# The first stretch of layer 0: x by single feature tiles, query products between key and value products

## The chip, the cores and the metric

The kernel runs on one core of one Trainium2 chip, in one launch. The metric is the time of one execution on the device, in microseconds (us); the number that is compared is the median of repeated executions. A profile of one execution lies beside the times: it gives the start and the length of every instruction on TensorE (PE, with its weight loads as PEld), VectorE (DVE), ScalarE (ACT), GpSimd (POOL) and SyncE (SP, which here only issues DMA transfers).

## The reference

Two layers of a decoder trunk over 512 tokens of 1024 features, in float32. The change touches only the beginning of layer 0, cut here to what it computes:

```python
h = _rms_norm(x, mix_norm[0])
q, k, v, cb, cc, cx = _split(h @ w_in, (512, 128, 128, 512, 512, 512))
q = _apply_rope(_rms_norm(q.reshape(b, s, 8, 64), q_norm), cos, sin)
k = _apply_rope(_rms_norm(k.reshape(b, s, 2, 64), k_norm), cos, sin)
attn = _sliding_window_sink_attention(q, k, v, sinks)
conv = cb * _causal_depthwise_conv(cc * cx, conv_w)
x = x + jnp.concatenate([attn, conv], axis=-1) @ w_out
```

The token's factor of the norm (one over its root mean square) is left out of h in the kernel and put on the finished products.

## The kernel before

Every float32 product is made of three matmuls in a rounded format: each operand is split into a rounded part (made by ACT, names `wh` for weights and the first `a` for x) and a rest (made by DVE, `wl` and the second `a`); rounded times rounded, rounded times rest and rest times rounded are summed in one PSUM bank. A helper `mm3` issues the three in a row.

In the first stretch of `mixer0`, x comes as rows of tokens (tiles `xin`) and has to be turned so that features lie on the partitions: PE transposes 128x128 blocks (against the identity, tile `cf`) into a PSUM bank, ACT and DVE read the bank for the two parts of the feature tile, and a third reading keeps x itself in `xT`. There are 8 feature tiles and 4 token tiles. For each feature tile k, the products of keys and values are 4 token tiles x 3 matmuls that give 128x256, those of queries 4 x 3 that give 128x512.

Before the change x is transferred in four pieces of two feature tiles, each as two transfers of 256 KB and followed by 256 KB of key and value weights, all on SP's queue. `features(c)` turns, splits and keeps the two tiles of piece c; `keys_values(k)` runs between them. The query weights come behind all that, as two transfers of 1 MB, and the 96 query matmuls run after the last `keys_values`. Ahead of it all, `idle` gives PE matmuls of ones into a bank that nobody reads: 7 in `setup`, 8 more after the first transposes.

Beside this PE work the chain of the keys runs on the other engines: the squares of x (L529) give the sums of the norm, POOL makes the factor `rtok` of each token (L209), ACT puts it on the key and value products (`kx` L570, `v` L574) and squares them (L543), DVE sums the squares (L545); the positions are turned by one small PE matmul (L418), DVE makes angles of them and, with ACT's sine, the tables `ropeS` and `ropeC` (L424 to L462); DVE combines them into the normed keys `kn` (L549, L554, L579). PE then transposes `kn` (L561), spreads `rtok` (L380) and starts the convolution's products.

Each engine works off its instructions in the order in which they stand. In the first stretch that order is the written one (`manual_schedule`) for PE, DVE and ACT; behind it a scheduler places the instructions of DVE and ACT. Weight tiles `wh` and `wl` have three buffers each, `raw` (weights as they come) has two: whoever writes a buffer again waits for its last reader. A queue's transfers are issued in order, and each waits until the transfer eight before it has landed.

## Time and profile before

| what | value |
|---|---|
| median of 3 runs | 1197.72 us (1196.88 to 1197.98) |
| profiled execution, own time | 1195.99 us |
| span of its instructions | 1194.0 us |
| granted TensorE clock over the span | 1.000 |
| PE from 8.0 to 22.9 us (keys and values) | 14.72 of 14.90 us busy |
| PE from 22.9 to 45.0 us (queries) | 22.10 of 22.10 us busy |
| first key product / first query product | 8.02 us / 23.04 us |
| kn's transposes on PE | 44.96 us |

Times inside the program are microseconds from the start of the span. A row of the timeline shows a start, a length (until the last result is written, so rows of one engine overlap), the engine, the line, the operation, the tile written and the tiles read, and in brackets how long the engine stood idle ahead of it and what ended that. PEq, ACTq, SPq and POOLq are the sequencers that issue transfers.

### The profile page before, as it was taken

Reading aid. Unit: us, or ns where it says so; the run is one execution under the profiler, and the core shown is the slowest. Engines: PE = TensorE matmul, PEld = TensorE weight load, DVE = VectorE, ACT = ScalarE, POOL = GpSimd, SP = SyncE. Lnnn points to the kernel's source line nnn. Section 1 sums busy time; section 2 is a strip of 40 time slices with the busy share of each in tenths; the row PEclk is TensorE's granted clock in tenths of the full one; section 3 lists DMA queues with packets and bytes.
Section 4 is the critical chain, followed back from the end, with each engine's and each line's share of the span. In section 5 each row is a group of like instructions: output and inputs, shape, how many; then the busy total and the mean of one; then the engine's idle time right before and its main releaser. Section 6 shows DMA issues by size and latency. Waiting matters only on the chain.

```text
span 1194.0 us, 20222 instructions
## 1 busy us (share of the span) xinstructions
PE 1187.1 (99%) x8218; PEld 1079.2 (90%) x8218; DVE 993.3 (83%) x1595; ACT 691.6 (58%) x1138; POOL 46.1 (4%) x64
## 2 busy tenths in 40 slices
PE   9999999999999999999999999999999999999998
PEld 8877789999999988889988988899999999888887
DVE  6786687898999987889879876688989999988595
ACT  7466565656565744756664655555555656655374
POOL 2610000000000000000100000000000000000000
PEclk9999999999999999999999999999999999999999
DMA  7222222333323343422412212223232333323601
GB/s 224 72 97 81 74 89 71 107 107 106 107 93 103 113 137 96 130 73 73 139 59 71 89 54 72 88 76 116 92 116 97 106 107 113 126 89 98 211 1 71
DMA packets 113072, 117.76 MB, mean 99 GB/s; under 512 B 2856, under 2 KB 108002, under 8 KB 112980
## 3 DMA queue, kind: packets, MB, share of 16 engines
q1 hardware_dynamic: 112144, 115.88, 29.8%
q8 instruction: 64, 1.05, 0.4%
q0 software_dynamic: 560, 0.42, 0.3%
q14 instruction: 28, 0.23, 0.1%
q10 hardware_dynamic: 276, 0.18, 0.1%
HBM read 114.37 MB, written 2.10 MB: 98 GB/s over the span
## 4 chain that ended last, share of the span: by engine, by line
PE 88%; DVE 8%; ACT 3%; issue 1%; DMA 0%; POOL 0%; ACTq 0%
PE ps L177 8%; PE ps L178 8%; PE ps L179 8%; PE pa L178 6%; PE pa L179 6%; PE pa L177 6%; PE ps L916 5%; PE ps L918 5%; PE ps L917 5%; PE ps L193 5%; PE ps L191 5%; PE ps L200 4%; PE pa L916 2%; PE pa L918 2%; PE pa L917 2%; DVE wl L864 2%
## 5 line engine op out<-in xcount | busy, mean ns | idle before, releaser
L153 DVE TENSOR_TENSOR wl<-raw,wh 128x1024 fp32r<-128x1024 f32 (+3 forms) x138 | 158.6, 1152 | 39.6 <-ACT wh L151 36.5
L151 ACT ACTIVATE wh<-raw 128x1024 fp32r<-128x1024 f32 (+4 forms) x142 | 140.9, 995 | 68.4 <-PE ps L178 26.3
L861 ACT ACTIVATE wh<-raw 128x1024 fp32r<-128x1024 f32 x90 | 95.7, 1063 | 129.5 <-DVE raw L888 79.0
L979 DVE SCALAR_TENSOR_TENSOR zt<-z,vfa,zt 128x510 f32<-128x510 f32 (+1 forms) x176 | 130.8, 744 | 0.3
L864 DVE TENSOR_TENSOR wl<-raw,wh 128x1024 fp32r<-128x1024 f32 x90 | 109.9, 1221 | 17.5 <-ACT wh L861 16.4
L179 PE MATMUL pa<-b,wl 128*128 128x256 f32 x352 | 97.3, 276 | 0.1
L179 PE MATMUL pa<-a,wl 128*128 128x256 f32 x352 | 97.2, 276 | 0.0
L177 PE MATMUL pa<-a,wh 128*128 128x256 f32 x352 | 97.2, 276 | 0.0
L177 PE MATMUL pa<-b,wh 128*128 128x256 f32 x352 | 97.2, 276 | 0.0
L178 PE MATMUL pa<-a,wh 128*128 128x256 f32 x352 | 97.2, 276 | 0.0
L178 PE MATMUL pa<-b,wh 128*128 128x256 f32 x352 | 97.2, 276 | 0.0
L977 ACT ACTIVATE zt<-z,vfb 128x512 f32<-128x512 f32 x88 | 71.3, 810 | 18.3 <-DVE z L969 8.7
L191 PE MATMUL ps<-b,wh 128*128 128x512 f32 (+1 forms) x192 | 73.0, 383 | 0.0
L193 PE MATMUL ps<-b,wh 128*128 128x512 f32 (+1 forms) x192 | 72.3, 379 | 0.0
L179 PEld LDWEIGHTS pa<-b,wl 128*128 128x128 f32 x352 | 66.1, 188 | 0.3 <-DVE wl L153 0.3
L177 PEld LDWEIGHTS pa<-a,wh 128*128 128x128 f32 x352 | 66.1, 188 | 0.0
L177 PEld LDWEIGHTS pa<-b,wh 128*128 128x128 f32 x352 | 66.1, 188 | 0.0
L178 PEld LDWEIGHTS pa<-b,wh 128*128 128x128 f32 x352 | 66.1, 188 | 0.0
L178 PEld LDWEIGHTS pa<-a,wh 128*128 128x128 f32 x352 | 66.1, 188 | 0.0
L179 PEld LDWEIGHTS pa<-a,wl 128*128 128x128 f32 x352 | 66.1, 188 | 0.0
L916 PE MATMUL ps<-four,wh 128*128 128x256 f32 x232 | 64.7, 279 | 0.0
L918 PE MATMUL ps<-four,wl 128*128 128x256 f32 x232 | 64.1, 276 | 0.0
(532 smaller groups left out, 3711.9 us busy)
## 6 DMA issues: line engine op xcount, KB each, us to landing
raw<-in_ffn_w_up_dram SPq DMA_DIRECT2D x42, 1024.0 KB, 5.1
raw<-in_ffn_w_down_dram SPq DMA_DIRECT2D x13, 1024.0 KB, 5.1
raw<-in_hy_w_in_dram SPq DMA_DIRECT2D x8, 1024.0 KB, 4.9
raw<-in_gla_w_in_dram SPq DMA_DIRECT2D x8, 1024.0 KB, 5.2
raw<-in_ffn_w_down_dram SPq DMA_DIRECT2D x8, 768.0 KB, 4.9
raw<-in_ple_w_gate_dram SPq DMA_DIRECT2D x6, 1024.0 KB, 6.5
raw<-in_hy_w_out_dram SPq DMA_DIRECT2D x16, 256.0 KB, 4.0
raw<-in_gla_w_out_dram SPq DMA_DIRECT2D x4, 1024.0 KB, 5.1
```

The source lines that it names most:

```text
L151: nc.scalar.activation(hv, v, AF.Copy)
L153: self.rest_cut = nc.vector.tensor_tensor(lv, v, hv.bitcast(F32), ALU.subtract)
L177: mm(out, lh, rh, start=start, stop=False, **kw)
L178: mm(out, lh, rl, start=False, stop=False, **kw)
L179: mm(out, ll, rh, start=False, stop=stop, **kw)
L191: mm(out, lh, rh, start=first, stop=False, **kw)
L193: end = mm(out, lt, rt, start=False, stop=False, **kw)
L861: nc.scalar.activation(h, src, AF.Copy)
L864: nc.vector.tensor_tensor(l, src, h.bitcast(F32), ALU.subtract)
L916: mm(out, wh, xh, start=first and j == 0, stop=False, **kw)
L918: mm(out, wl, xh, start=False, stop=j == ND // 2 - 1, **kw)
L979: nc.vector.scalar_tensor_tensor(out=y[:, tap:], in0=z[:, : S - tap], scalar=w[:, f : f + 1], in1=y[:, tap:], op0=ALU.mult, op1=ALU.add,)
```

## The change

x comes by one feature tile for the first two tiles (transfers of 128 KB) and by two after that. Weights for queries of the first four feature tiles come on the same queue between the pieces of x, 256 KB for a single tile and 512 KB for two. The first 128 KB of key and value weights are issued by ACT, right behind the identity; the gain vector, which ACT issued, is now issued by POOL. The query products of feature tiles 0 to 3 run between the key and value products; those of tiles 4 to 7 stay behind them. The three matmuls of a product are no longer issued in a row but in passes over the four token tiles. The turned tiles share two PSUM banks, where each had one of four in turn. The idle matmuls are 4 and 3 where they were 7 and 8. Two of the four squares of x stand earlier. What is computed is the same.

```diff
--- before.py
+++ after.py
@@ -217,14 +217,16 @@
         self.ident = self.cf[:, :P]
         self.ones = self.cp.tile([P, P], F32, name="ones")
         self.ones_r = self.sp.tile([P, S + 64], F32R, tag="sq", name="ones_r", bufs=2)[:, :P]
-        self.nowhere = self.pa()
+        self.nowhere = self.ps()
+        self.kvr = self.raw(ND, 256)
         with self.tc.manual_schedule(engines={ET.PE, ET.DVE, ET.Activation}):
             nc.vector.memset(self.ones, 1.0)
             nc.vector.tensor_copy(self.ones_r, self.ones)
             nc.vector.memset(self.mhalf, -0.5)
             nc.scalar.dma_start(self.ident, a["cst_f"][:, :P])
+            nc.scalar.dma_start(self.kvr[:, 0, :], a["hy_w_in"][0][:P, 512:768])
             self.vec0 = self.load_vectors0()
-            self.idle(7)
+            self.idle(4)
         self.invf = self.cf[:, P + 32 : P + 64]
         self.amask = self.cf[:, P + 64 :]
 
@@ -265,7 +267,7 @@
     def load_vectors0(self):
         a = self.a
         f = lambda v: v.rearrange("i (k p) -> (i k) p", p=P)
-        finish = self.columns("vec0", [f(a["mix_norm"])], self.nc.scalar)
+        finish = self.columns("vec0", [f(a["mix_norm"])], self.nc.gpsimd)
 
         def turned():
             v = finish()
@@ -468,65 +470,169 @@
             w_in = a["hy_w_in"][0].rearrange("(k p) n -> p k n", p=P)
             self.xT = [self.xp.tile([P, S], F32, name=f"xT{m}") for m in range(ND)]
             xin = [mp.tile([P, 2, D], F32, tag="s", name=f"xin{u}", bufs=2) for u in range(2)]
-            kvr = self.raw(ND, 256)
-            for c in range(4):
-                cols = slice(c * 256, (c + 1) * 256)
+            kvr, wqr = self.kvr, self.raw(4, 512)
+            load = nc.sync.dma_start
+
+            def load_x(m0, m1):
+                cols = slice(m0 * P, m1 * P)
                 for u in range(2):
                     rows = a["x"][0, u * 256 : (u + 1) * 256, cols]
-                    nc.sync.dma_start(xin[u][:, :, cols], rows.rearrange("(t p) d -> p t d", p=P))
-                nc.sync.dma_start(kvr[:, 2 * c : 2 * c + 2, :], w_in[:, 2 * c : 2 * c + 2, 512:768])
+                    load(xin[u][:, :, cols], rows.rearrange("(t p) d -> p t d", p=P))
+
+            def load_kv(k0, k1):
+                load(kvr[:, k0:k1], w_in[:, k0:k1, 512:768])
+
+            def load_q(k0, k1):
+                load(wqr[:, k0:k1], w_in[:, k0:k1, :512])
+
+            load_x(0, 1)
+            load_q(0, 1)
+            load_x(1, 2)
+            load_kv(1, 2)
+            load_q(1, 2)
+            load_x(2, 4)
+            load_kv(2, 4)
+            load_x(4, 6)
+            load_q(2, 4)
+            load_kv(4, 6)
+            load_x(6, 8)
+            load_kv(6, 8)
             self.gate = xin[1][:, 1, D - 1 :]
             self.late(self.cf[:, P + 32 : P + 33])
             nc.gpsimd.dma_start(self.cf[:, P + 32 :], a["cst_f"][:, P:])
 
             xg = self.xg = []
             tok = lambda k, t: (xg[k][0][:, t * P : (t + 1) * P], xg[k][1][:, t * P : (t + 1) * P])
+            turns = [self.pa(), self.pa()]
             pkv = [self.pa() for _ in range(2)]
             pkv = [pkv[t // 2][:, (t % 2) * 256 : (t % 2) * 256 + 256] for t in range(NT)]
-            wkv = []
-
-            def keys_values(k):
-                for t in range(NT):
-                    self.mm3(
-                        pkv[t], tok(k, t), wkv[k // 2](k % 2, 0, 256),
-                        start=k == 0 and t % 2 == 0, stop=k == ND - 1 and t % 2 == 1,
-                    )
-
-            def features(c, fill=0):
-                ms = (2 * c, 2 * c + 1)
-                pss = [self.ps() for _ in ms]
-                for u in range(2):
-                    if c == 0 and u == 1:
-                        self.vec0()
-                    for m, ps in zip(ms, pss):
-                        for t in (2 * u, 2 * u + 1):
-                            nc.tensor.transpose(
-                                ps[:, t * P : (t + 1) * P], xin[u][:, t % 2, m * P : (m + 1) * P], self.ident
-                            )
-                self.idle(fill)
-                for m, ps in zip(ms, pss):
-                    hl = self.pair(self.fp, "a0", "a1")
-                    self.split(hl, ps, self.g_mix[0][:, m : m + 1])
-                    xg.append(hl)
-                    if m == (c > 0) + 2 * c:
-                        wkv.append(self.cut(kvr[:, 2 * c : 2 * c + 2, :], "a"))
-                return [
-                    copy(self.xT[m], ps) for m, ps, copy in zip(ms, pss, (nc.scalar.copy, nc.vector.tensor_copy))
-                ]
-
-            with tc.manual_schedule(engines={ET.PE, ET.DVE, ET.Activation}):
-                features(0, 8)
-                for c in range(1, 4):
-                    keys_values(c - 1)
-                    last = features(c)
-                for k in range(3, ND):
-                    keys_values(k)
-            wq = [self.weights(w_in[:, k0 : k0 + 4, :512], 4, 512, by="a") for k0 in (0, 4)]
+            psq = [self.ps() for _ in range(NT)]
+            wkv, wq = {}, {}
             sums = self.few(NT, "ss")
             junk = mp.tile([P, D], F32, tag="pT", name="junk")
+            passes = ((0, 0), (1, 0), (0, 1))
+
+            def keys_values(k, *ns):
+                for n in ns:
+                    u, v = passes[n]
+                    for t in range(NT):
+                        nc.tensor.matmul(
+                            pkv[t], tok(k, t)[u], wkv[k][v],
+                            start=k == n == 0 and t % 2 == 0, stop=k == ND - 1 and n == ns[-1] and t % 2 == 1,
+                        )
+
+            def queries(k, *ns):
+                for n in ns:
+                    u, v = passes[n]
+                    for t in range(NT):
+                        nc.tensor.matmul(
+                            psq[t], tok(k, t)[u], wq[k][v], start=k == n == 0, stop=k == ND - 1 and n == ns[-1]
+                        )
+
+            def turn(*ms):
+                for m in ms:
+                    for t in range(NT):
+                        nc.tensor.transpose(
+                            turns[m % 2][:, t * P : (t + 1) * P],
+                            xin[t // 2][:, t % 2, m * P : (m + 1) * P], self.ident,
+                        )
+
+            def rounded_x(m):
+                xg.append(self.pair(self.fp, "a0", "a1"))
+                nc.scalar.activation(xg[m][0], turns[m % 2], AF.Copy, scale=self.g_mix[0][:, m : m + 1])
+
+            def rest_x(m):
+                h, l = xg[m]
+                nc.vector.scalar_tensor_tensor(
+                    out=l, in0=turns[m % 2], scalar=self.g_mix[0][:, m : m + 1], in1=h.bitcast(F32),
+                    op0=ALU.mult, op1=ALU.subtract,
+                )
+
+            def rounded_w(parts, raw, k0, tiles):
+
+                n, w = raw.shape[1:]
+                h, l = (x[:, : n * w].rearrange("p (a b) -> p a b", b=w) for x in tiles)
+                nc.scalar.activation(h, raw, AF.Copy)
+                parts.update({k0 + q: (h[:, q], l[:, q]) for q in range(n)})
+                return lambda: nc.vector.tensor_tensor(l, raw, h.bitcast(F32), ALU.subtract)
+
+            def kept(m, copy):
+                return copy(self.xT[m], turns[m % 2])
+
+            def square(t):
+                nc.scalar.activation(junk, xin[t // 2][:, t % 2, :], AF.Square, accum_out=sums[:, t : t + 1])
+
+            on_act, on_dve = nc.scalar.copy, nc.vector.tensor_copy
+            part = lambda tiles, c0, c1: [x[:, c0:c1] for x in tiles]
+            with tc.manual_schedule(engines={ET.PE, ET.DVE, ET.Activation}):
+                kv01, q01 = self.weight_tiles(), self.weight_tiles()
+                turn(0)
+                self.vec0()
+                self.idle(3)
+                rounded_w(wkv, kvr[:, 0:1], 0, part(kv01, 0, 256))()
+                rounded_x(0)
+                rest_x(0)
+                keys_values(0, 0, 2, 1)
+                rounded_w(wq, wqr[:, 0:1], 0, part(q01, 0, 512))()
+                rest = rounded_w(wkv, kvr[:, 1:2], 1, part(kv01, 256, 512))
+                kept(0, on_act)
+                queries(0, 0)
+                turn(1)
+                rounded_x(1)
+                rest()
+                rest_x(1)
+                rounded_w(wq, wqr[:, 1:2], 1, part(q01, 512, 1024))()
+                kept(1, on_dve)
+                queries(0, 1, 2)
+                keys_values(1, 0, 1, 2)
+                rest = rounded_w(wkv, kvr[:, 2:4], 2, self.weight_tiles())
+                queries(1, 0)
+                turn(2, 3)
+                rounded_x(2)
+                rounded_x(3)
+                rest()
+                rest_x(2)
+                rest_x(3)
+                kept(2, on_act)
+                kept(3, on_dve)
+                queries(1, 1, 2)
+                keys_values(2, 0, 1, 2)
+                rests = [
+                    rounded_w(wkv, kvr[:, 4:6], 4, self.weight_tiles()),
+                    rounded_w(wq, wqr[:, 2:4], 2, self.weight_tiles()),
+                ]
+                turn(4, 5)
+                rounded_x(4)
+                rounded_x(5)
+                for rest in reversed(rests):
+                    rest()
+                rest_x(4)
+                rest_x(5)
+                kept(4, on_act)
+                kept(5, on_dve)
+                keys_values(3, 0, 1, 2)
+                queries(2, 0, 1, 2)
+                rest = rounded_w(wkv, kvr[:, 6:8], 6, self.weight_tiles())
+                square(0)
+                square(1)
+                keys_values(4, 0, 1, 2)
+                turn(6, 7)
+                rounded_x(6)
+                rounded_x(7)
+                rest()
+                rest_x(6)
+                rest_x(7)
+                last = [kept(6, on_act), kept(7, on_dve)]
+                keys_values(5, 0, 1, 2)
+                queries(3, 0)
+                keys_values(6, 0, 1, 2)
+                keys_values(7, 0, 1, 2)
+                queries(3, 1, 2)
+            wq47 = self.weights(w_in[:, 4:8, :512], 4, 512, by="a")
+            wq.update({k: wq47(k - 4, 0, 512) for k in range(4, ND)})
             with tc.issue_after(last[0].ins):
-                for t in range(NT):
-                    nc.scalar.activation(junk, xin[t // 2][:, t % 2, :], AF.Square, accum_out=sums[:, t : t + 1])
+                square(2)
+                square(3)
             self.end_norm(sums=sums)
             with tc.issue_after(last[1].ins):
                 C, Sn = self.rope_tables(mp)
@@ -578,10 +684,9 @@
             kn = mp.tile([P, 8, HD], F32, tag="qn", name="kn", bufs=2)
             nc.vector.tensor_tensor(kn, m1, rk.unsqueeze(2).to_broadcast([P, 8, HD]), ALU.mult)
 
-            psq = [self.ps() for _ in range(NT)]
-            for k in range(ND):
+            for k in range(4, ND):
                 for t in range(NT):
-                    self.mm3(psq[t], tok(k, t), wq[k // 4](k % 4, 0, 512), start=k == 0, stop=k == ND - 1)
+                    self.mm3(psq[t], tok(k, t), wq[k], start=False, stop=k == ND - 1)
             turned(kn, kT, nc.vector.tensor_copy, self.pa)
             qTs = []
 
```

The order of the instructions at three places that are spoken of below.

**PE, from its first instruction to the first key and value product.** `ones_r` holds ones, `cf` the identity, `vrow` the gain vector, `wh`, `wl` and `a` as above. Before:

```order
L235 MATMUL pa_80<-ones_r 128x512 x7
L503 MATMUL ps_132<-cf,xin_111 128x128 x2
L503 MATMUL ps_133<-cf,xin_111 128x128 x2
L259 MATMUL pa_138<-cf,vrow_87 128x16
L503 MATMUL ps_132<-cf,xin_112 128x128 x2
L503 MATMUL ps_133<-cf,xin_112 128x128 x2
L235 MATMUL pa_80<-ones_r 128x512 x8
L177 MATMUL pa_128<-wh_157,a_11_153 128x256
```

And now:

```order
L237 MATMUL ps_80<-ones_r 128x512 x4
L535 MATMUL pa_132<-cf,xin_110 128x128 x2
L535 MATMUL pa_132<-cf,xin_111 128x128 x2
L261 MATMUL pa_152<-cf,vrow_89 128x16
L237 MATMUL ps_80<-ones_r 128x512 x3
L519 MATMUL pa_134<-wh_144,a_21_160 128x256 x2
L519 MATMUL pa_135<-wh_144,a_21_160 128x256 x2
```

Four transposes, one feature tile, stand where eight stood, and seven idle matmuls where fifteen stood.

**PE, around the transpose of the positions** (`pos_f`). Before:

```order
L178 MATMUL pa_129<-wl_270,a_37_265 128x256
L179 MATMUL pa_129<-wh_269,a_38_266 128x256
L418 MATMUL pa_371<-cf,pos_f 128x4
L177 MATMUL ps_448<-wh_338,a_11_153 128x512
L178 MATMUL ps_448<-wl_339,a_11_153 128x512
```

And now:

```order
L528 MATMUL ps_138<-wl_266,a_29_234 128x512
L528 MATMUL ps_139<-wl_266,a_29_234 128x512
L420 MATMUL pa_418<-cf,pos_f 128x4
L177 MATMUL ps_136<-wh_399,a_35_276 128x512
L178 MATMUL ps_136<-wl_400,a_35_276 128x512
```

It stood ahead of all 96 query products; now 48 of them (tiles 0 to 3) stand ahead of it and 48 behind it. Then come the transposes of `kn`, before and now.

**ACT, from the last squares of x to the squares of the keys.** `wh` with `raw` is the rounding of query weights, `kx` and `v` the key and value products with the token's factor. Before:

```order
L529 ACTIVATE junk,ss_356<-xin_112 128x1024 [waits Activation_49]
L151 ACTIVATE wh_348<-raw_346 128x1024 [waits DMAHW7_49,DVE_49,PE_49]
L570 ACTIVATE kx<-pa_128,rtok_362 128x128 [waits Pool_49]
L574 ACTIVATE v_422<-pa_128,rtok_362 128x128
L570 ACTIVATE kx<-pa_128,rtok_362 128x128
```

And now:

```order
L563 ACTIVATE junk,ss_140<-xin_111 128x1024 [waits Activation_49]
L151 ACTIVATE wh_403<-raw_397 128x1024 [waits PE_49]
L676 ACTIVATE kx<-pa_134,rtok_409 128x128 [waits PE_49,Pool_49]
L680 ACTIVATE v_469<-pa_134,rtok_409 128x128
L676 ACTIVATE kx<-pa_134,rtok_409 128x128
```

The places are the same, but the rounding ahead of `kx` now writes the buffer that held the query weights of tiles 2 and 3, whose last reader is the last matmul of `queries(3, 1, 2)`, right ahead of the positions' transpose on PE; before, it wrote a buffer of key and value weights. On DVE the sum of the squared keys (L545, now L651) stood in the middle of the cosine's steps and now stands in the sine's, ahead of its third step. From the transposes of `kn` on, the order of PE is as before, and from the scores of the first query block on, that of all engines.

## The prediction

> **What bounds the kernel now.** I read the page first, then the busy time by stretches, the timeline of PE over the first 45 us, and the timelines of ACT, DVE and POOL up to the keys' transposes.
>
> ```profile
> span 1194.0 us, 20222 instructions
> PE 1187.1 (99%) x8218; PEld 1079.2 (90%) x8218; DVE 993.3 (83%) x1595; ACT 691.6 (58%) x1138; POOL 46.1 (4%) x64
> PE 88%; DVE 8%; ACT 3%; issue 1%; DMA 0%; POOL 0%; ACTq 0%
> ```
>
> ```profile
> 8.00:22.90 14.90, 14.72 (x122) 1.00 0.84 257
> 22.90:45.00 22.10, 22.10 (x99) 1.00 0.37 120
> ```
>
> PE sets the time: it is busy 99% of the span and 88% of the chain that ended last. In the touched stretch it stands still for 0.18 us of 37 (first column the stretch, then its length and PE's busy time). So nothing is to be won there except what PE does that is of no use, and that lies ahead of 8 us:
>
> ```profile
> 1.31 3.35 PE L235 MATMUL pa<-ones_r 128*128 128x512 f32 x7 [1.31 <-DVE mhalf L224]
> 4.47 1.05 PE L503 MATMUL ps<-cf,xin 128*128 128x128 f32 x4
> 5.45 0.28 PE L259 MATMUL pa<-cf,vrow 16*128 16x16 f32 x1
> 5.67 0.66 PE L503 MATMUL ps<-cf,xin 128*128 128x128 f32 x4
> 6.08 2.10 PE L235 MATMUL pa<-ones_r 128*128 128x512 f32 x8
> 8.02 0.28 PE L177 MATMUL pa<-wh,a 128*128 128x256 f32 x1
> ```
>
> The first useful product starts at 8.02 us. PE changes its pace between 5.45 and 6.1 us: seven idle matmuls take 3.35 us, later eight take 2.10; four transposes take 1.05, then 0.66.
>
> **The change part by part.** First the start.
>
> ```profile
> 0.73 0.45 ACTq L225 DMA_DIRECT2D cf<-in_cst_f_dram  x1
> 4.28 0.84 PEld L503 LDWEIGHTS ps<-cf,xin 128*128 128x128 f32 x4 [0.33 <-DMA cf<-in_cst_f_dram]
> 5.77 0.17 DVE L260 COPY vec<-pa 128x16 f32<-128x16 f32 x1 [4.49 <-PE pa L259]
> 6.15 0.69 ACT L113 ACTIVATE a<-ps,vec 128x512 fp32r<-128x512 f32 x1 [2.92 <-PE ps L503]
> cf<-in_cst_f_dram ACTq DMA_DIRECT2D x1, 64.0 KB, 3.2
> xin<-in_x_dram SPq DMA_DIRECT2D x8, 256.0 KB, 5.1
> ...
> vrow<-in_ffn_norm_dram POOLq DMA_DIRECT2D x1, 8.0 KB, 3.0
> ```
>
> The identity is issued at 0.73 as before and lands 3.2 us later, so transposes cannot start before about 4.2. The second half of tile 0 is issued 0.48 us behind the first and holds 128 KB: between the 3.2 us of 64 KB and the 5.1 of 256 KB it lands between 4.4 and 6.3. I take 4.4, because the 5.1 is a median over eight transfers of which most stood in a queue. From the first transpose at 4.47 to the end of the gain copy (5.77 + 0.17) were 1.47 us; that piece, four transposes and the gain, is unchanged. Then the rounding of x: 4.4 + 1.5 + 0.7 = 6.6 us for the first key product, 1.4 earlier than 8.02. Early bound 6.2, late bound 7.2. The three idle matmuls end by about 6.5 and cost nothing. The gain vector, now POOL's, has until 5.3; by the last row 8 KB from POOL land 3.0 us after issue, so by 4.2 (POOL is free from 0.73). The first key weights, 128 KB behind the identity on ACT's queue, stand ahead of the rounding of x on ACT and are issued at about 1.2; at 5.1 us they would land at 6.3 and delay the start by 0.4, which the late bound holds.
>
> Next the pace of the products.
>
> ```profile
> 8.61 0.27 PE L177 MATMUL pa<-wh,a 128*128 128x256 f32 x1
> 9.55 0.28 PE L179 MATMUL pa<-wh,a 128*128 128x256 f32 x1
> 9.68 1.03 PE L503 MATMUL ps<-cf,xin 128*128 128x128 f32 x8
> 22.89 0.22 PE L418 MATMUL pa<-cf,pos_f 4*128 4x4 f32 x1
> 44.96 0.60 PE L561 MATMUL pa<-cf,kn 128*128 128x128 f32 x4
> ```
>
> Eight starts in 0.94 us make 0.119 us for a 128x256 product; transposes are 0.109 apart (eight in 1.03 with the last one's tail of 0.27); the 96 query products fill 22.89 + 0.15 to 44.96, 0.228 each. From the first key product to the positions' transpose PE now does 96 x 0.119 + 28 x 0.109 + 48 x 0.228 = 11.4 + 3.1 + 10.9 = 25.4 us. Passes over four banks instead of three matmuls into one cost nothing by these rows, since products into one bank and into the next are equally far apart. Weights and x come in time: by the queue's rows 256 KB take 0.7 us at the 370 GB/s of
>
> ```profile
> GB/s 0 0 0 0 0 93 157 153 369 374 378 388 366 369 377 344 341 298 251 208 229 243 339 380 385 380 374 377 388 374 391 402 418 410 399 415 410 371 191 148
> ```
>
> (40 slices of 0.375 us), the 1.9 MB up to the tiles 2 and 3 are there at about 8.5 us and are turned after 13; all 4.2 MB are there at about 15, and the last are turned after 24. The five added issues on SP, 0.5 us each, lie inside that. So the positions' transpose stands at Z = 6.6 + 25.4 = 32.0 us, and the 48 query products left end at 32.0 + 0.15 + 10.95 = 43.1, 1.9 us ahead of 44.96. That is the gain if nothing waits.
>
> But the keys' chain now starts late. Its rows before:
>
> ```profile
> 24.51 1.05 POOL L209 TENSOR_TENSOR rtok<-rs,mhalf 128x4 f32<-128x4 f32 x1 [5.30 <-DVE rs L208]
> 24.13 1.04 ACT L151 ACTIVATE wh<-raw 128x1024 fp32r<-128x1024 f32 x1
> 25.59 0.37 ACT L570 ACTIVATE kx<-pa,rtok 128x128 f32<-128x128 f32 x1 [0.42 <-POOL rtok L209]
> 27.27 1.28 ACT L444 ACT_TABLE_LOAD   x1
> 28.56 0.31 ACT L444 ACTIVATE tabsin<-tabsin 128x128 f32<-128x128 f32 x1
> 29.28 0.63 ACT L543 ACTIVATE m<-kx 128x512 f32<-128x512 f32 x1
> 29.80 1.05 ACT L151 ACTIVATE wh<-raw 128x1024 fp32r<-128x1024 f32 x1
> 23.18 0.15 DVE L420 COPY cf<-pa 128x4 f32<-128x4 f32 x1
> 28.91 0.29 DVE L459 SCALAR_TENSOR_TENSOR ropeS<-gqk,tabsin 128x128 f32<-128x128 f32 x1 [1.43 <-ACT tabsin L444]
> 30.46 0.68 DVE L545 TENSOR_REDUCE ss<-m 128x8 f32<-128x512 f32 x1
> 31.94 1.21 DVE L153 TENSOR_TENSOR wl<-raw,wh 128x1024 fp32r<-128x1024 f32 x1
> 33.08 0.28 DVE L457 TENSOR_TENSOR ropeC<-gqk,tabcos 128x128 f32<-128x128 f32 x1
> 35.59 0.69 DVE L579 TENSOR_TENSOR kn<-m,rq 128x512 f32<-128x512 f32 x1
> ```
>
> Before, kn was done at 36.3, 8.7 us ahead of its transposes: that cover is used up. Now two things hold the chain back to Z: the positions are turned only there, and ACT's rounding of the last query weights waits for the last product of tile 3, with `kx` behind it in ACT's order. From Z on: 0.2 for that product's own end and 1.0 for the rounding (Z + 1.2); eight evacuations at 0.25, as 25.59 to 27.27 shows for six of them (Z + 3.2); the squares 0.63 (Z + 3.9). DVE, which has the angles ready by then, stands at the sum of squares, 0.6, then 0.5 of small steps (Z + 5.0), the rest of the convolution's weights 1.15 (31.94 to 33.08; their rounding on ACT, 1.05 behind the squares, is just done), 0.9 for the sine's last steps, 0.35 for ACT's sine (Z + 7.4; the table load, 1.28, hides behind DVE). Then the rope steps 1.55 (28.91 to 30.46), 0.6 for the two last cosine steps, 1.15 for the second rest, and from the first `ropeC` to the end of kn 35.59 + 0.69 - 33.08 = 3.2: Z + 13.9. POOL's parts fit beside it. So kn is there at 45.9, and PE, done at 43.1, stands 2.8 us still, with the spreading of `rtok` and all the convolution's products behind the waiting transposes. Those transposes start at 45.9 instead of 44.96: 1.0 us later than before. Bounds of the chain: 0.7 shorter, if the small steps and one rest overlap better, 0.7 longer. Nothing behind it moves on its own: the first query block's scores have work of over 10 us in between, so the shift is carried to the end. The profiled execution took 1195.99 us, 1.7 less than the median of the runs; I add the 1.0 to the median: 1198.7 us.
>
> **The rivals.** (a) The clock comes late, and the kernel is slower. Before, PE worked from 1.31 us without a hole of more than 0.2 us and sped up some 4.3 us later. Seven idle matmuls filled 1.31 to 4.47, 0.45 each, so the four now end near 3.1, and nothing runs until 4.4. If the count begins anew there, the pace changes at 4.4 + 4.3 = 8.7: the three idle matmuls, 0.45 each from 5.6 on, then push the first product to 6.9, and 1.8 us run at half pace, 0.9 lost. Together 1.2 more, which the keys' chain, hanging on Z, passes on in full: 2.2 over before, 1199.9 us. It decides from a pause that resets the count; no row of before has such a pause. [...] The trace agrees with a delay of some 4 us before the pace changes (1.31 to 5.45 or later); what a pause does, it does not show.
>
> (b) The keys' chain is shorter than I make it, or its rows overlap, and PE never waits: the full 1.9 us are won, 1195.9 us; with the early bound of the start, 6.2, it is 2.3. For it speaks that the chain's length is added up from rows of another order; against it that two independent waits both start it at Z, and that it would have to be 2.8 us shorter.
>
> (c) x or the first weights are late (6.3 instead of 4.4 us for tile 0): 1.9 us later start, all of it passed on, 2.9 over before, 1200.6 us. The dip to 208 GB/s at 7 us speaks for a little of that.
>
> **How the numbers follow.** The forecast has a chance of 0.50, 1198.7 us, its own range 1197.7 to 1199.8. (a) 0.30, 1199.9; (b) 0.12, 1195.9; (c) 0.08, 1200.6. The range for 8 in 10 reaches from 1195.8, just beyond (b), to 1201.0, beyond (a) and (c) with part of their bounds. About what a measurement of this kernel can tell from no change is 0.2%, 2.4 us: 1195.3 to 1200.1. Slower than that: half of (a), nearly all of (c) and the late end of the forecast, 0.15 + 0.07 + 0.03 = 0.25. Faster: the better part of (b) with an early start, 0.05. Within: 0.70.
>
> **What would show it.** Right: the first key product near 6.6, the positions' transpose near 32, a hole on PE of 2 to 3 us ahead of the keys' transposes, put down to DVE's `kn`, and those at 45.9. Query products spaced 0.228 from tile 0 on and transposes 0.109 apart after 6 us speak against (a); products at 0.2 and 0.4 us up to 8.7 or 9 for it. No hole ahead of the keys' transposes means (b), and a wait for `xin` or `raw` in the first 10 us means (c). The forecast is wrong if the hole is under 1 us or the positions' transpose comes after 33.

## The result, and the profile after

| | median, us | lowest to highest | executions | ratio to before, 95% interval |
|---|---|---|---|---|
| before | 1196.97 | 1195.35 to 1198.20 | 11 | |
| after | 1200.29 | 1197.56 to 1201.66 | 11 | 1.0022 (1.0013 to 1.0032) |
| after, timed once more on the same chip as the last experiment | 1199.88 | 1197.90 to 1201.52 | 12 | 1.0017 (1.0008 to 1.0025) |

By the ratios, which go by the means of the executions, the change makes the kernel some 2.0 to 2.6 us slower (0.0017 and 0.0022 of 1197); the medians lie 3.3 and, against the 1197.81 of before that was timed beside it, 2.1 us apart. The forecast was 1.0 us slower, 1198.7 us.

The first lines of the page of after, and of its part on the chain that ended last, beside those of before:

```profile
span 1195.8 us, 20221 instructions
PE 1186.5 (99%) x8210; PEld 1077.5 (90%) x8210; DVE 995.1 (83%) x1597; ACT 693.6 (58%) x1140; POOL 46.2 (4%) x65
...
PE 86%; DVE 8%; ACT 3%; DMA 1%; issue 1%; POOL 0%; ACTq 0%; DVEq 0%
```

PE still sets the time. It works 0.6 us less and the span is 1.8 us longer, so it stands still more. The timeline of PE in after shows where:

```profile
1.31 2.07 PE L237 MATMUL ps<-ones_r 128*128 128x512 f32 x4 [1.31 <-DVE mhalf L225]
3.76 1.21 PE L535 MATMUL pa<-cf,xin 128*128 128x128 f32 x4 [0.37 <-DMA xin<-in_x_dram]
5.11 1.65 PE L237 MATMUL ps<-ones_r 128*128 128x512 f32 x3
6.55 1.04 PE L519 MATMUL pa<-wh,a 128*128 128x256 f32 x4
...
32.64 0.22 PE L420 MATMUL pa<-cf,pos_f 4*128 4x4 f32 x1
...
43.57 0.39 PE L179 MATMUL ps<-wh,a 128*128 128x512 f32 x1
46.10 0.66 PE L667 MATMUL pa<-cf,kn 128*128 128x128 f32 x4 [2.14 <-DVE kn L685]
46.95 0.47 PE L177 MATMUL ps<-a,wh 128*128 128x512 f32 x1
```

and two rows of before:

```profile
44.73 0.39 PE L179 MATMUL ps<-wh,a 128*128 128x512 f32 x1
...
45.75 0.48 PE L177 MATMUL ps<-a,wh 128*128 128x512 f32 x1
```

The first key product starts 1.5 us earlier than before (6.55 against 8.02), the last query product starts 1.16 us earlier (43.57 against 44.73), and then PE stands 2.14 us waiting for `kn`. Its transposes come 1.14 us later than before, the convolution's first product 1.20 (46.95 against 45.75).

This profiled execution took 1197.56 us, the shortest of its eleven, with a mean granted clock of 1.000 (the granted clock is the share of TensorE's full clock that it was given). In the 23 timed executions of after the mean clock divides the times: 8 executions at 1.000 took 1197.6 to 1198.7 us, 12 at 0.998 and 3 at 0.999 took 1199.1 to 1201.7. None of the 85 executions of before that were timed beside the experiments below shows 0.998, but 35 of them show 0.999, so 0.999 alone tells little. So the profile above shows a part of the loss only.

### The profile page after: what moved, and what is told of

It is laid out like the page before. It is cut to its first block, busy times and chain, and to the rows that moved or that the text cites. A ratio compares the mean times of both kernels' runs of the same rounds, so it can differ in the third digit from the quotient of the medians.

```text
span 1195.8 us, 20221 instructions
## 1 busy us (share of the span) xinstructions
PE 1186.5 (99%) x8210; PEld 1077.5 (90%) x8210; DVE 995.1 (83%) x1597; ACT 693.6 (58%) x1140; POOL 46.2 (4%) x65
## 4 chain that ended last, share of the span: by engine, by line
PE 86%; DVE 8%; ACT 3%; DMA 1%; issue 1%; POOL 0%; ACTq 0%; DVEq 0%
PE ps L177 7%; PE ps L178 7%; PE ps L179 7%; PE pa L179 6%; PE pa L178 6%; PE pa L177 6%; PE ps L1021 5%; PE ps L1023 5%; PE ps L1022 5%; PE ps L193 5%; PE ps L191 5%; PE ps L200 4%; PE pa L1023 2%; PE pa L1021 2%; PE pa L1022 2%; DVE wl L969 2%
## 5 line engine op out<-in xcount | busy, mean ns | idle before, releaser
L153 DVE TENSOR_TENSOR wl<-raw,wh 128x1024 fp32r<-128x1024 f32 (+2 forms) x132 | 153.8, 1168 | 35.9 <-ACT wh L151 33.7
L151 ACT ACTIVATE wh<-raw 128x1024 fp32r<-128x1024 f32 (+3 forms) x136 | 136.7, 1007 | 64.1 <-PE ps L178 26.9
```

Of the source, the lines that this page charges most:

```text
L151: nc.scalar.activation(hv, v, AF.Copy)
L153: self.rest_cut = nc.vector.tensor_tensor(lv, v, hv.bitcast(F32), ALU.subtract)
```

## The experiments

Each kernel was timed beside the kernel before on the same chip. Medians of before in the three batches were 1197.13 (the first four experiments), 1197.43 (the fifth to the eighth) and 1197.81 us (the last two).

**1. The pause at the start filled.** Idle matmuls add nothing to the output; six instead of four cover the time until x is there.

```diff
-            self.idle(4)
+            self.idle(6)
```

> The changed kernel with 6 idle matmuls ahead of the first transposes where it has 4, so that PE has no pause of a microsecond before x lands. Clock theory (the pause makes the clock come later, or drop again, in most executions): executions with a mean granted clock below 1.000 vanish, and the median falls by 1.5 to 2.5 us from 1200.3, to about 1198.3. Keys' chain theory alone (the loss is only PE's wait for kn): the hole ahead of the keys' transposes stays at 2 to 2.5 us and the median stays at 1200.3 within 0.7.

Measured: 1199.34 us, ratio 1.0018 (1.0010 to 1.0027). That is 0.95 us below the first median of after, but the intervals of the two ratios overlap. Neither theory had that: the one expected 1.5 to 2.5 us and no mean clock below 1.000 (four of the eleven executions are at 0.998 and three at 0.999), the other no change beyond 0.7. The first key product came at 6.24 us and the granted clock was full from 4.30 us, against 7.46 in the profile of after. The gain did not reach the end, as the timeline of PE shows:

```profile
28.61 0.74 PE L519 MATMUL pa<-wh,a 128*128 128x256 f32 x4 [0.77 <-DVE a L546]
...
47.30 0.66 PE L667 MATMUL pa<-cf,kn 128*128 128x128 f32 x4 [2.95 <-DVE kn L685]
48.15 0.48 PE L177 MATMUL ps<-a,wh 128*128 128x512 f32 x1
48.71 0.63 PE L179 MATMUL ps<-a,wl 128*128 128x512 f32 x1
49.14 0.63 PE L177 MATMUL ps<-a,wh 128*128 128x512 f32 x1
```

At 28 us PE waited 0.77 us for VectorE, which stood behind its multiply on the sinks (that waited for its transfer until 27.73 us). The hole ahead of `kn` grew to 2.95 us, and behind it stood something that the profile of after does not have: from 48.7 us the convolution's products start 0.43 us apart instead of 0.23. The same kernel by stretches (length, busy time and count of PE, PEld, DVE, ACT and POOL, then the granted clock, the share of DMA and GB/s):

```profile
45.27:48.68 3.41, 1.38 (x10) 1.31 (x11) 3.24 (x6) 2.02 (x3) 1.90 (x3) 1.00 0.74 261
48.68:52.09 3.41, 3.41 (x9) 2.64 (x8) 3.41 (x6) 1.30 (x3) 3.41 (x3) 0.50 0.00 0
```

For 3.41 us the granted clock was half, though the mean over this execution reads 0.999. From the transposes of `kn` to the first scores PE took 16.15 us (47.30 to 63.45) where it took 14.53 in after (46.10 to 60.63): 1.6 us lost. This was the new theory: the hole itself costs some 1 us, as was forecast, and the clock that falls behind it costs more than as much again.

**2. The positions turned early.** Their cast and transpose move into the written order, the transpose between the products of tiles 6 and 7.

```diff
                 last = [kept(6, on_act), kept(7, on_dve)]
+                nc.vector.tensor_copy(pos_f, pos_i)
...
                 keys_values(6, 0, 1, 2)
+                self.turn_positions(pos_f, turns[0])
                 keys_values(7, 0, 1, 2)
```

> The changed kernel with the transpose of the positions on PE between the key and value products of feature tiles 6 and 7, some 3.3 us earlier; everything else stays. Keys' chain theory: PE's hole ahead of the keys' transposes shrinks from 2.4 us to under 0.6, and the median falls by 1.9 to 2.4 us, to about 1198. Clock theory alone, or a chain that is held by the evacuations of the key and value products and not by the positions: the hole and the median stay within 0.7 us.

Measured: 1197.10 us, ratio 1.0000 (0.9991 to 1.0009), no execution at 0.998. The timeline of PE:

```profile
43.71 0.39 PE L179 MATMUL ps<-wh,a 128*128 128x512 f32 x1
44.96 0.63 PE L675 MATMUL pa<-cf,kn 128*128 128x128 f32 x4 [0.86 <-DVE kn L693]
```

With nothing moved but the positions, the wait fell from 2.14 to 0.86 us, the transposes of `kn` stood where they stood before the change, and the whole loss was gone. The keys' chain is held by the positions, but not by them alone: their transpose came 3.10 us earlier than in after (29.54 against 32.64), and `kn` was done only 1.23 us earlier (44.81 against 46.04). So the wait shrank less than was expected (under 0.6 us), while the median fell by 3.2 us, more than the expected 1.9 to 2.4, which left out the clock behind the hole.

**3. Both.** Experiment 2 with the six idle matmuls of experiment 1.

> Both edits, 6 idle matmuls ahead and the positions' transpose between tiles 6 and 7. If both theories hold, the two gains add up: 3.5 to 4.5 us below the changed kernel, 1196.3 or less, as fast as the kernel before or up to 1 us faster, with all executions at a clock of 1.000. If only one holds, about 1198.

Measured: 1196.97 us, ratio 0.9997 (0.9989 to 1.0005). The transposes of `kn` came at 44.24 us, with a wait of 0.80 us ahead of them. It is 3.3 us below the first median of after, where 3.5 to 4.5 were expected: filling the start added no more than 0.13 us to what the positions gave, so the two gains did not add up. One execution of twelve was at 0.998 (1200.37 us), where none was expected; what happened in it was not profiled.

**4. The pause alone, in the kernel before.** Four idle matmuls in `setup` instead of seven, nothing else.

```diff
-            self.idle(7)
+            self.idle(4)
```

> The kernel before with 4 idle matmuls ahead of its first transposes where it has 7, and nothing else changed; its first transposes wait for the identity until about 4. Clock theory: part of its executions show a mean clock below 1.000 and the median rises by 1 to 2.5 us over the kernel before. Without an effect of the pause: the same time as the kernel before within 0.5 us, or up to 0.4 less, as transposes start earlier.

Measured: 1198.40 us, ratio 1.0007 (0.9999 to 1.0016); 1.27 us by the medians, not certain by the interval. The timeline of PE is plain:

```profile
1.31 2.08 PE L235 MATMUL pa<-ones_r 128*128 128x512 f32 x4 [1.31 <-DVE mhalf L224]
4.14 1.09 PE L503 MATMUL ps<-cf,xin 128*128 128x128 f32 x4 [0.75 <-DMA xin<-in_x_dram]
...
6.14 3.76 PE L235 MATMUL pa<-ones_r 128*128 128x512 f32 x8
9.70 0.41 PE L177 MATMUL pa<-wh,a 128*128 128x256 f32 x1
```

Eight idle matmuls take 3.76 us where they took 2.10, and the first key product starts at 9.70 instead of 8.02. The granted clock was full from 10.11 us, against 5.65. So three idle matmuls fewer, and the pause of 0.75 us that they leave, put off the full clock by 4.46 us in these two profiles, and the positions' transpose by 1.63 (24.52 against 22.89). The mean clock doesn't show this: the record begins when the clock is first full (here at 10.11 us), and the clock column of the stretches reads 1.00 from 5 to 10.11 us too, while PE works at about half pace (3.76 us against 2.10).

**5. The positions ahead of tile 4, and the sink's copy out of the way.** Experiment 3, with the cast and the transpose moved further ahead, and VectorE's multiply on the sinks (which stood ahead of tiles 6 and 7 and waited for its transfer) put behind the last tile.

```diff
+                nc.vector.tensor_copy(pos_f, pos_i)
+                self.turn_positions(pos_f, turns[0])
                 keys_values(4, 0, 1, 2)
...
-            nc.vector.tensor_scalar_mul(sink, sink, -1.0)
+            with tc.issue_after(last[1].ins):
+                nc.vector.tensor_scalar_mul(sink, sink, -1.0)
```

> As the third experiment (positions turned early, six idle matmuls at the start), but with the positions turned already ahead of the fifth feature tile's key and value products, and the multiply on the sink's copy put behind the last feature tile on VectorE, so that no wait of VectorE for that copy stands ahead of the positions. Theory of the keys' chain (the hole ahead of the transposes of kn is where the time of the change goes, its length is set by when VectorE's cosines and sines are done): kn is done before the last query product ends, the hole of 1.2 us goes below 0.4 us, the first convolution product starts at about 44.2 us instead of 45.1, and the median is 1196.0 to 1196.5 us, 0.5 to 1 us below the kernel before. Rival (the end is set by something later, such as the queries' second half or the weights of the convolution, and what is won at 45 us is given back): the hole goes, the median stays at that of the third experiment, 1197.0. Third possibility: VectorE's work in front of the fifth tile's copies delays the copies of tiles and TensorE stalls among the projections instead, 1197.5 or more.

Measured: 1195.93 us, ratio 0.9992 (0.9983 to 1.0001). The timeline of PE:

```profile
43.64 0.39 PE L179 MATMUL ps<-wh,a 128*128 128x512 f32 x1
43.87 0.60 PE L676 MATMUL pa<-cf,kn 128*128 128x128 f32 x4
...
58.01 0.40 PE L179 MATMUL ps<-a,wl 128*128 128x512 f32 x1
58.90 1.29 PE L745 MATMUL pa<-kT,qT 64*128 64x128 f32 x16 [0.49 <-ACT qT L677]
```

The hole is gone, and the transposes come 1.1 us earlier than before the change. Half of that is given back at the first scores, which now wait for the turned queries: they start 0.52 us earlier than before, where the row is

```profile
59.42 1.16 PE L631 MATMUL pa<-kT,qT 64*128 64x128 f32 x16
```

The interval only just takes in no change, which is why this kernel was timed again (9).

**6. The hole filled.** Ten idle matmuls between the last query product and the transposes of `kn`; the keys' chain is not touched.

```diff
+            self.nowhere = self.pa()
+            with tc.manual_schedule(engines={ET.PE}):
+                self.idle(10)
             turned(kn, kT, nc.vector.tensor_copy, self.pa)
```

> The changed kernel with ten idle matmuls of 512 columns (about 0.22 us each at full clock, 2.2 us in all) put on TensorE between the last query product and the transposes of kn, into a bank of their own; the keys' chain is untouched, so the transposes of kn start where they did, at 46.1 us in the profile, and the work left out is none. Theory that a part of the loss is the clock (the hole of 2.5 us makes the granted clock fall to half for 3.41 us behind it in most executions, which costs about 1.7 us there): the fall goes, executions with a mean clock of 0.998 to 0.999 become rare, and the median falls from 1200.3 by 1.3 to 2 us to 1198.3 to 1199.0. Rival (the clock of the first 10 us, which this does not touch, spreads the executions): the share of executions at 0.998 stays and the median is 1200 or more. Rival that the keys' chain alone costs 2.6 us: 1200.0 to 1200.5, a mean clock below 1.000 as often as before.

Measured: 1199.19 us (1198.26 to 1199.96), ratio 1.0014 (1.0005 to 1.0023), no execution at 0.998. The timeline of PE:

```profile
44.52 0.39 PE L179 MATMUL ps<-wh,a 128*128 128x512 f32 x1
44.75 2.43 PE L237 MATMUL pa<-ones_r 128*128 128x512 f32 x10
47.02 0.63 PE L667 MATMUL pa<-cf,kn 128*128 128x128 f32 x4
47.85 0.48 PE L177 MATMUL ps<-a,wh 128*128 128x512 f32 x1
```

The useful work starts as late as ever, but the fall of the clock is gone: 0 of 11 executions at 0.998 against 12 of 23, and the clock column of this profile reads 1.00 from 47.00 to 50.41 us, behind the filled hole. The median is 0.7 to 1.1 us below the two of after, by the ratios 0.4 to 1.0, which is less than the 1.3 to 2 that were expected; the intervals of the ratios overlap, so it is the clock that shows this, and the size in time is less certain.

**7. Both stretches filled**, experiment 6 with experiment 1.

> The sixth experiment with six idle matmuls instead of four at the start too, so that both stretches in which TensorE has nothing to do are filled. If the hole's clock and the start's clock both cost time in the changed kernel: the start gives about 0.9 us as in the first experiment (1200.3 to 1199.3 there) on top of what the hole gives, and the median is 1197.3 to 1198.2. If the first experiment's 0.9 us came from the same fall of the clock that the sixth removes, the two don't add up and the median is that of the sixth, within 0.4 us. No execution with a mean clock below 0.9995 is expected either way, by the theory of the clock.

Measured: 1198.63 us, ratio 1.0010 (1.0001 to 1.0019), no execution at 0.998, though six were at 0.999, against what was expected; but before has 0.999 as well, and the profile of experiment 4 shows 0.999 with no fall but the one behind the program's last matmuls. It is 0.56 us less than experiment 6, where 0.9 was expected. In the profiles the positions' transpose came 1.46 us earlier than in experiment 6 (32.13 against 33.59) and the transposes of `kn` 0.61 us (46.41 against 47.02), so less than half of an earlier start came through. With both stretches filled the loss is 1.2 us, and this is what the keys' chain costs as it runs in this kernel.

**8. After, profiled again.** This kernel is the changed one.

> The changed kernel, unaltered, profiled once more: its first profile was taken of an execution that was the fastest of eleven, with a mean clock of 1.000, where eight of the eleven had 0.998 or 0.999. Theory of the clock: if this execution has a mean clock of 0.998 or 0.999 its time is 1199 to 1201.7 us, and its record of the granted clock shows 3.41 us at about half right behind the hole of 2.5 us, between 46 and 53 us, with the first convolution products 0.43 us apart instead of 0.23. Rival: the slower clock lies in the first 12 us (the full clock comes one step of 3.41 us later, the first key product at 7 us or later), and there is no fall behind the hole.

Measured: 1201.20 us, mean clock 0.998. Both halves of the expectation were there, not one or the other. The timeline of PE, and the same by stretches:

```profile
3.68 1.33 PE L535 MATMUL pa<-cf,xin 128*128 128x128 f32 x4 [0.29 <-DMA xin<-in_x_dram]
...
9.16 1.55 PE L528 MATMUL ps<-wh,a 128*128 128x512 f32 x4
...
47.22 0.71 PE L667 MATMUL pa<-cf,kn 128*128 128x128 f32 x4 [2.03 <-DVE kn L685]
48.43 0.78 PE L177 MATMUL ps<-a,wh 128*128 128x512 f32 x1
49.00 0.63 PE L178 MATMUL ps<-a,wh 128*128 128x512 f32 x1
```

```profile
44.28:47.69 3.41, 1.38 (x9) 0.88 (x8) 3.27 (x4) 1.39 (x3) 2.72 (x3) 1.00 0.95 281
47.69:51.11 3.42, 3.42 (x12) 2.87 (x11) 3.38 (x7) 2.30 (x4) 3.31 (x4) 0.50 0.08 26
```

At the start the four query products from 9.16 us take 1.55 us, where later 1.09 are enough (in the first profile): the clock was full only from 10.15 us, and the positions' transpose came at 33.87. Behind the hole the clock fell to half for 3.42 us. From the transposes of `kn` to the first scores it took 16.12 us (47.22 to 63.34), 1.6 more than in the first profile.

**9 and 10. The fifth kernel and the changed one timed once more**, on one chip.

> The fifth experiment's kernel once more, unaltered, since its interval (0.9983 to 1.0001 of the kernel before) only just takes in no change. Theory: with no hole ahead of the transposes of kn it is 0.5 to 1.5 us faster than the kernel before, a ratio of 0.9988 to 0.9996, most executions between 1195 and 1197 us. Rival: the first eleven executions were lucky, the kernel equals the third experiment's, ratio 0.9996 to 1.0002.

> The changed kernel, unaltered, timed once more beside runs of the kernel before on the same chip, to see how firm its loss is and how many executions have the slower mean clock. Theory of the two losses (keys' chain in all executions, the clock behind the hole in most): ratio 1.0017 to 1.0027, two thirds or more of the executions at a mean clock of 0.998 or 0.999 and 1199 to 1202 us, the rest at 1.000 and 1197.5 to 1199 us. Rival (the share of such executions was chance, or the chip's): fewer than a third of them at 0.998, ratio 1.0008 to 1.0015, near the 1.0010 that was forecast.

Measured: the fifth kernel 1196.01 us, ratio 0.9984 (0.9975 to 0.9993): faster than before, by a little more than the 0.9988 to 0.9996 that were expected. The changed kernel 1199.88 us, ratio 1.0017 (1.0008 to 1.0025), six of twelve executions at 0.998 and one at 0.999; "two thirds or more" was a little too many. In its profile, which was again at 1.000, the positions' transpose came at 33.21 us, that of `kn` at 46.55 us, and there was no fall.

## Why the prediction was right, and where it was short

**The number: right by its wide range, and in part by luck.** 1200.29 us lies within 1195.8 to 1201.0, the range that took in all rivals, but outside the forecast's own 1197.7 to 1199.8. The forecast added 1.0 us to 1197.72, a median of three; the eleven executions of before have 1196.97. Measured beside before, the loss was 2.0 to 2.6 us, at least twice the forecast and close to the 2.2 of rival (a), though not by (a)'s sum either.

**The place and the size of the wait: right.** Forecast: PE done with the query products at 43.1 us, a hole of 2 to 3 us put down to DVE's `kn`, transposes at 45.9. Measured in the first profile: last product started at 43.57, 2.14 us of waiting, 46.10; in the other two profiles of the changed kernel 2.03 and 2.01 us of waiting, and the transposes at 47.22 and 46.55. That the first came so close to 45.9 is two errors that cancel, as the next paragraphs show: the chain began later and was shorter than forecast. Experiments 2 and 5 show the cause: with the positions earlier, the hole shrinks and goes, and with it the loss.

**What holds the chain: half wrong.** Two things were said to hold it to the positions' transpose, Z. The positions do. The rounding of the last query weights on ACT does not; the timeline of after, PE with ACT and DVE:

```profile
29.26 1.12 PE L519 MATMUL pa<-wh,a 128*128 128x256 f32 x8
30.70 1.09 PE L528 MATMUL ps<-wh,a 128*128 128x512 f32 x4
...
30.34 0.18 ACT L563 ACTIVATION_READ_ACCUMULATOR junk<-xin 128x1 f32 x1
30.43 1.05 ACT L151 ACTIVATE wh<-raw 128x1024 fp32r<-128x1024 f32 x1
31.90 0.37 ACT L676 ACTIVATE kx<-pa,rtok 128x128 f32<-128x128 f32 x1 [0.41 <-POOL rtok L209]
...
32.89 0.16 DVE L422 COPY cf<-pa 128x4 f32<-128x4 f32 x1 [0.15 <-PE pa L420]
45.35 0.69 DVE L685 TENSOR_TENSOR kn<-m,rq 128x512 f32<-128x512 f32 x1
```

The rounding ran at 30.43, right behind the squares and ahead of the query products at 30.70 that still read rounded weights. So the buffer that it writes cannot be that of the query weights of tiles 2 and 3, as the section on the change has it; it starts as the reading of rounded key and value weights (29.26 + 1.12) ends. `kx` waited for `rtok`. That is why one move, of the positions, took the loss away. What holds the chain next is this path over the squares, `rtok` and `kx`, and DVE's slow products while POOL works (last section): in experiment 7, with the positions at 32.13, DVE stood 0.57 us waiting for ACT's squares of the keys, and two `ropeC` products took 0.83 and 0.82 us instead of 0.28. No experiment moved these two.

**The chain's length: nearly right.** Forecast Z + 13.9 us; measured 45.35 + 0.69 - 32.64 = 13.4. Z itself came at 32.64 instead of 32.0. From the first key product to Z it was 26.1 us, not 25.4. About half of that is the clock, which was full only from 7.46 us, so that four key products went at about half pace (0.86 us, from 6.55 to 7.41, where four from 7.91 on took 0.47); the rest is the sum, since experiment 7, at full clock from 5.04 us on, took 25.8 (6.36 to 32.13).

**The first product: right**, 6.55 us against 6.6 (6.60 and 6.76 in the other two profiles), and after the first transposes x and the weights held PE up nowhere in the first 60 us. Rival (c) is out. Rival (b) is out too.

**The start at full clock: wrong.** The forecast took the clock's pace as before; rival (a) had it late. In three profiles of the changed kernel it was full from 7.46, 8.54 and 10.15 us, against 5.65 in that of before, and the positions' transpose followed at 32.64, 33.21 and 33.87: against the first profile 0.57 and 1.23 us for delays of 1.08 and 2.69, about half of each, as fits the half pace above. The prediction called itself wrong if the positions' transpose comes after 33 us; in two of the three profiles it does. Over all runs, six profiles in which the pause was filled (before, and experiments 1, 3, 5, 7 and 9) had it full from 4.30 to 7.29 us, six with the pause (the three of after, experiments 2, 4 and 6) from 7.46 to 10.15. So the late clock of rival (a) was there (in the kernel before too: 10.11 us in experiment 4), and its times are those of the middle profile: full clock at 8.7 us, first key product at 6.9 and so the positions at 33.2 were forecast, and 8.54, 6.76 and 33.21 measured. Where (a) was wrong is that the keys' chain passes this on in full: experiments 6 and 7 put the cost at the end at some 0.5 us, not 1.2.

Whether it is the pause itself that holds the clock back, or something else in the time ahead, was not separated. PE's busy time alone does not tell the two cases apart. These are the 3.41 us up to the rise of the clock in experiment 1, at 4.30 us, and 3.41 us in the eighth run, up to 6.73, behind which it did not rise until 10.15 (length, PE's busy time and count, then the clock column, which reads 1.00 here in any case, the share of DMA and GB/s):

```profile
0.89:4.30 3.41, 2.98 (x8) 1.00 0.66 176
3.32:6.73 3.41, 3.12 (x10) 1.00 0.93 258
```

**The step that failed: "Nothing behind it moves on its own".** The sum stopped at the moment when the transposes start. It took PE's pace behind the hole as given, though rival (a) reasoned on just that for a pause in the first microseconds. A term is missing: behind the hole the granted clock fell to half (0.50 for 3.42 us in the eighth run, for 3.41 in experiment 1), 1.6 us lost in each of these two profiles. By the mean clock, 12 to 15 of the 23 executions have such a fall (12 at 0.998, three more at 0.999 and 1199.1 us or longer): an estimate, since only two of the 23 were profiled, and those had none. That the hole does it is shown by experiment 6, where it is filled and nothing else is changed: no execution of 11 at 0.998.

The sum as it should have been: keys' chain 1.2 us (forecast 1.0), start 0.5, fall 1.6 us in 12 to 15 of 23 executions, 0.8 to 1.0 on the mean. Together 2.5 to 2.7 us; the two ratios give 2.6 and 2.0. The second and third term rest on medians whose intervals overlap, so they are known to about half a microsecond; that the late rise and the fall both occur is shown by the records of the clock (full from 7.46 to 10.15 us against 5.65; 0.50 behind the hole).

## What to carry to other kernels

A wait on TensorE was paid twice here, in the two profiles where the 3.41 us that held most of it had 1.38 us of work (next section): price a hole of some 2 us with the clock behind it, not only with its length, and look at the mean granted clock of all executions, since one profile may have missed the fall. When work is moved ahead of a chain, move the small instruction that starts the chain ahead with it: here one transpose of 0.22 us decided between 2 us lost and nothing lost (experiment 2). Moved further still, with six idle matmuls and the sink's multiply out of the way, some 1 to 2 us were won. Ten idle matmuls in the hole saved the clock here (no execution of 11 at 0.998) but not the hole: the transposes of `kn` stood at 47.02 us, against 46.10 to 47.22 without them (experiment 6).

## What was not expected of the hardware

**The falls of the clock came a whole number of 3.41 us after its rise.** So it was with both falls behind the hole: 47.69 - 10.15 = 37.5 = 11 x 3.41 in the eighth run, 48.68 - 4.30 = 44.4 = 13 x 3.41 in the first experiment. The full clock up to the fall at the end of the kernel has such lengths too: 1187.84 us both in before (from 5.65) and in the first profile of after (from 7.46), 348 times 3.413, and 1184.42 us in experiment 4 (10.11 to 1194.53), 347 times. Laid out with that step from the rise on, the first and the last profile of after had the hole cut in two by a boundary between two stretches. The stretches up to and behind that boundary, in the first:

```profile
41.59:45.00 3.41, 2.37 (x11) 1.63 (x9) 3.27 (x7) 2.01 (x3) 2.04 (x2) 1.00 0.44 126
45.00:48.42 3.42, 2.32 (x15) 2.07 (x16) 3.35 (x6) 2.28 (x4) 2.85 (x3) 1.00 0.51 181
```

and in the last:

```profile
42.67:46.09 3.42, 1.86 (x9) 1.21 (x7) 3.25 (x8) 1.88 (x3) 2.09 (x3) 1.00 0.59 178
46.09:49.50 3.41, 2.95 (x17) 2.61 (x18) 3.38 (x6) 2.64 (x4) 3.30 (x3) 1.00 0.37 129
```

No stretch there has less than 1.86 us of work, and no fall follows; in the two profiles with a fall the stretch ahead of it had 1.38 us, 40% of it. So of two holes of the same length one was followed by the fall (2.03 us of waiting, eighth run) and one was not (2.01, last profile); they differ in how they lie in that step. That this is why the executions divide in two is an estimate from these four profiles. (The means of the 8 at 1.000 and of the 12 at 0.998 lie 2.4 us apart, more than 1.6; the one profile of the changed kernel with the fall is also the one with the latest start.) The end of the kernel, where PE runs out of work, gives two more such stretches. The last one with work in experiment 4, and in experiment 7:

```profile
1191.12:1194.53 3.41, 1.46 (x13) 1.00 0.20 71
...
1189.47:1192.88 3.41, 1.62 (x14) 1.00 0.27 94
```

The clock fell at 1194.53 in the one, right behind 1.46 us of work; in the other not behind 1.62, but one stretch later, behind none. In before and in the first profile of after, laid out in the same way (348 stretches each), the clock fell only behind the last one (at 1193.49 and 1195.30 us), which held no work of PE; the least that any of the others held was 3.06 us and 2.32 us. So in the stretches named here the clock fell behind 0, 1.38 and 1.46 us of work in 3.41 us, and not behind 1.62 and more; none of them lies between 1.46 and 1.62.

**DVE while POOL works.** In the timeline of after, DVE's products of 128x512, 0.69 us in `kn`, take 1.0 to 1.1 while POOL works on `m`:

```profile
43.08 1.11 DVE L655 TENSOR_TENSOR m<-kx,ropeC 128x512 f32<-128x512 f32 x1
44.29 1.02 DVE L660 TENSOR_TENSOR m<-m,m 128x512 f32<-128x512 f32 x1
...
42.73 2.04 POOL L657 TENSOR_TENSOR m<-q,ropeS 128x256 f32<-128x256 f32 x2 [1.71 <-ACT q L695]
```

The late chain thus also met POOL's work on the queries, which it used to be ahead of: before, POOL's first work on `q` waited 9.2 us for ACT, until after `kn`. The two products were 0.75 us longer together than two of 0.69, at the end of the chain. In the profile of experiment 7, where POOL's work was over at 43.87 us, the same two products (at 44.05 and 44.85) took 0.69 each, and the `ropeC` products beside POOL were the slow ones. That POOL is the cause was not tried by an experiment of its own.
